# The second token mixer: latents and rotary terms worked in PSUM, squares summed by products alone, and a later begin of GpSimd's share

## The chip, the cores and the metric

The kernel runs on one core of one Trainium2 chip. The metric is the device time of the whole program in microseconds (us). A core has five engines that matter here: TensorE (PE, matrix products, with its weight loads as PEld), VectorE (DVE), ScalarE (ACT), GpSimd (POOL), and SyncE (SP), whose queue issues the loads of the weights. SBUF is the large on-chip memory that all of them use; PSUM holds what TensorE writes, in eight banks of 128 partitions x 512 fp32 values, and VectorE and ScalarE can read and write it too.

## The reference, cut to what matters

256 tokens of width 1024 go through two blocks of a network. The change lies in the token mixer of the second block:

```python
def token_mixer(h, cos, sin, w_in, conv_w, conv_b, conv_norm_g, conv_norm_b, w_conv_out,
                q_norm_g, w_uq, kv_norm_g, w_ukv, w_attn_out, w_out):
    z = h @ w_in                       # 2048 + 384 + 256 + 64 + 2048 columns
    u_glu, q_lat, kv_lat, k_r, gate_logits = jnp.split(z, IN_SPLIT, axis=-1)
    ua, ub = jnp.split(u_glu, 2, axis=-1)
    u = causal_depthwise_conv(ua * jax.nn.sigmoid(ub), conv_w, conv_b)      # 31 taps
    u = jax.nn.silu(layer_norm(u, conv_norm_g, conv_norm_b))
    y_a = u @ w_conv_out
    q = (rms_norm_2(q_lat, q_norm_g) @ w_uq).reshape(...)                   # 8 heads, 128 + 64
    kv = (rms_norm_2(kv_lat, kv_norm_g) @ w_ukv).reshape(...)
    q_rope, k_rope = apply_rope(q_rope, cos, sin), apply_rope(k_r, cos, sin)
    o = mla_attention(q_nope, q_rope, k_nope, k_rope, v)
    y_b = o @ w_attn_out
    g_a, g_b = jnp.split(jax.nn.sigmoid(gate_logits), N_BRANCHES, axis=-1)
    return (g_a * y_a + g_b * y_b) @ w_out
```

`rms_norm_2` of a latent needs, for each token, the sum of its squares over the latent's width (384 or 256); the layer norm needs the sum and the sum of squares over 1024.

## The kernel before, in words

All activations lie with the features on the 128 partitions and the 256 tokens along the row, so a latent of width 384 is three tiles of 128x256, one of 256 is two.

**Weights.** Every weight is cut into tiles of 128x128, eight tiles to a chunk of 512 KB, loaded one chunk at a time by SyncE's queue. Each chunk is split (`Weights.split`, L185 and L186) into a high part `hi` (ScalarE) and a low part `lo` = raw - hi, made either by VectorE or by GpSimd: `ws.share` is the share of chunks whose `lo` GpSimd takes. Each tile then gives three products of 256 columns: xl by hi, xh by lo, xh by hi, where xh and xl are the two parts of the activations. The helpers `mm` (L365), `act` (L362), `stt` (L353), `tt` (L350), `ts` (L357, L359) record every operation under their own lines.

**Order.** Code is written in one stream and a scheduler orders each engine's queue by it. `after(n, fn)` puts `fn` behind n more weight tiles; a list of background work, the 8 x 31 taps of the convolution, is dealt out at 0.8 taps to a weight tile (`TAP_RATE`). A tap is one VectorE operation that adds into a PSUM bank (tile `cva`; the last of a block of channels writes `cv` to SBUF).

**The mixer** (`mixer2`). Three blocks of the gated part are first multiplied with unmodulated activations (`gemm_fold`), while the modulation (tile `mod`, on VectorE, then `xh` on ScalarE and `xl` on VectorE, L353) is prepared. Then come the 48 weight tiles of the latents: two banks with two latent tiles each, and a third with the last latent tile and the rotary part of the keys. `epi_lat` copies each bank to SBUF (`lat`, `krt`). After the third bank ScalarE squares the latents (`lsq`), GpSimd adds the squares of the three and of the two tiles (L1566), and `lat_stats`, 20 tiles later (`AFTER_LAT`), sums them over the partitions with products by a column of ones (tile `sums`) and works two chains of small VectorE operations for the reciprocal roots. `lat_bc`, 56 tiles after, spreads these over the partitions (tile `dg`, product `bcps`, copy `bc` in SBUF), multiplies the latents (`lat`) and splits them into `lath` (ScalarE) and `latl` (VectorE). Meanwhile TensorE works at the 80 tiles of the rest of the gated part. The products with w_uq and w_ukv need `lath` and `latl`. The rotary terms of the keys and of two pairs of query blocks go through `rope_pair`: a product by a permutation (tile `rope`), times sin into `rt`, the source times cos in place, and their sum (`krt`, `qr`).

**Attention** follows by heads: scores (`att`), the causal mask added by a product, the maximum on VectorE (`mx`), exponentials on ScalarE, `rc` and `p` on VectorE or ScalarE, a transpose (`pt`), a copy (`pT`), and the product with the values (`o`); the products of the gate (`gate`) stand between the heads. Last, the **layer norm** of the convolved tile `cv` runs beside the gate's products: `ln2` subtracts the mean, squares four tiles of 128x512 (`Sums.square`, ScalarE), adds them on GpSimd (L262), folds the rest on VectorE and sums by two products. fp32 products (the sums, `bcps`) have two records each in the trace.

Of the kernel before, what the change touches and what calls it, by code (L numbers as in the profile page):

```python
# [9 lines left out]
F32 = mybir.dt.float32  # L10
# [4 lines left out]
AF = mybir.ActivationFunctionType  # L15
ALU = mybir.AluOpType
AX = mybir.AxisListType

P = 128
T = 256  # L20
# [7 lines left out]
EPS = 1e-6  # L28
# [8 lines left out]
AFTER_ROPE = 4  # L37
# [9 lines left out]
SC_ATT = 1.0 / math.sqrt(192.0)  # L47
# [225 lines left out]
class Kern:  # L273
# [1176 lines left out]
    def mixer2(self, xs, sums, nxt):  # L1450
        nc = self.nc
        h = self.h
        flat = lambda ap: ap.rearrange("p a t -> p (a t)")
        v2 = lambda ap: ap.rearrange("p (a t) -> p a t", a=2)
        half = lambda ps, m: ps[:, (m % 2) * T:(m % 2 + 1) * T]
        rope = {}
# [5 lines left out]
        lat = {}  # L1462
# [15 lines left out]
        latp = self.slot("lat", (P, 5, T))  # L1478
        lath, latl = self.slot("lath", (P, 5, T), F32R), self.slot("latl", (P, 5, T), F32R)
        krt = self.slot("krt", (P, 3, T))  # L1480
# [7 lines left out]
        for k in range(KD):  # L1488
            self.modulate(k, xs, self.gs[:, k:k + 1], bc4, self.shift1)

        def epi_lat(j, ps):
            if j < 2:
                self.act(latp[:, 2 * j:2 * j + 2, :], v2(ps), AF.Copy)
            else:
                self.act(latp[:, 4, :], ps[:, 0:T], AF.Copy)
                self.act(krt[:, 0, :], ps[:, T:2 * T], AF.Copy)


        up = [self.slot("up", (P, 4, 32 + T)) for _ in range(2)]
# [46 lines left out]
        for m in range(NFOLD):  # L1546
            za, zb = self.mid("za", (P, T)), self.mid("zb", (P, T))
            for j, z in ((1, zb), (0, za)):
# [2 lines left out]
            self.act(za, za, AF.Identity, bias=bias[:, 2 * m:2 * m + 1])  # L1551
            glu(m, zb, za)
        self.bg_rate = TAP_RATE
        self.ws.share = 1.0
        self.gemm(X, range(KD), [[lambda k, c=c: win(k, c) for c in (2048, 2176)],
                                 [lambda k, c=c: win(k, c) for c in (2304, 2432)],
                                 [lambda k: win(k, 2560), kr_src]], epi_lat, kouter=2)
        lsq, lsqt = {}, self.slot("lsq", (P, 5, T))
        for nm, a, n in (("q", 0, 3), ("kv", 3, 2)):
            lsq[nm] = flat(lsqt[:, a:a + n, :])  # L1560
            self.act(lsq[nm], flat(latp[:, a:a + n, :]), AF.Square)

        for nm, n in (("q", 3), ("kv", 2)):
            for i in range(1, n):
                o = lsq[nm][:, 0:T]
                nc.gpsimd.tensor_tensor(out=o, in0=o, in1=lsq[nm][:, i * T:(i + 1) * T], op=ALU.add)  # L1566

        def lat_stats():
            for nm, n in (("q", 3), ("kv", 2)):
                lat[nm] = self.rstd_tok([lsq[nm][:, 0:T]], n * P, EPS)  # L1570

        def lat_bc():
            bcs = [self.bcast(lat[nm], act=True) for nm in ("q", "kv")]
            for bc, a, n in zip(bcs, (0, 3), (3, 2)):
                for i in range(a, a + n):
                    g = self.pv("qn", i) if i < 3 else self.pv("kvn", i - 3)
                    z = latp[:, i, :]
                    self.stt(z, z, g, bc, ALU.mult, ALU.mult)
                    self.split(lath[:, i, :], latl[:, i, :], z)

        self.after(AFTER_LAT[0], lat_stats)
        self.after(AFTER_LAT[1], lat_bc)

        def x2(k):
# [8 lines left out]
        qn, qr = self.slot("qn"), self.slot("qr", (P, 4, T))  # L1593
# [9 lines left out]
            a = 2 * (i - 8)  # L1603
            return ("w_uq_2", 0, k * P, P, 0, ((a * 192 + 128, 64), ((a + 1) * 192 + 128, 64)))

        def rope_pair(dst, src, n):

            ps = self.bank("rope")
            for i in range(n):
                self.mm(ps[:, i * T:(i + 1) * T], self.cst("perm", 128), src[:, i, :])  # L1610
            t = self.mid("rt", (P, 2, T,), F32)
            cb = lambda a: a.unsqueeze(1).to_broadcast([P, n, T])
            self.tt(t[:, 0:n, :], ps[:, 0:n * T].rearrange("p (a t) -> p a t", a=n), cb(rope["sin"]), ALU.mult)
            self.tt(src, src, cb(rope["cos"]), ALU.mult)
            self.tt(dst, src, t[:, 0:n, :], ALU.add)

        def epi_qr(j, ps):
            t = self.mid("qrt", (P, 2, T,), F32)
            self.act(t, v2(ps), AF.Copy, scale=SC_ATT)
            self.after(AFTER_ROPE, lambda: rope_pair(qr[:, 2 * j:2 * j + 2, :], t, 2))  # L1620

        rope_pair(krt[:, 1:2, :], krt[:, 0:1, :], 1)
        kr = krt[:, 1, :]
        self.gemm(L(0), range(3), [[lambda k, i=i: uq(k, i) for i in (2 * j, 2 * j + 1)] for j in range(4)],
                  copied(qn, SC_ATT), kouter=0)
        self.gemm(L(0), range(3), [[lambda k, i=i: uq(k, i) for i in (8 + 2 * j, 9 + 2 * j)] for j in range(2)],
                  epi_qr, kouter=0)
        self.gemm(L(3), range(2), [[lambda k, i=i: full("w_ukv_2", 0, k, i * 256) for i in (2 * j, 2 * j + 1)]
                                   for j in range(4)], copied(kn), kouter=0)
# [111 lines left out]

        def ln2():
            mb = self.bcast(ln["mu"])
            sm = Sums(self)
            for j in range(4):
                c = cv[:, 2 * j:2 * j + 2, :]
                self.tt(c, c, self.rb(mb), ALU.subtract)
                sm.square(flat(c))
            ln["sm"] = sm
# [14 lines left out]
        for n, f in zip(AFTER_LN, (ln1, ln2, ln3, ln4)):  # L1764
            self.after(n, f)
# [351 lines left out]
```

## Time and profile before

| | |
|---|---|
| median of 3 runs | 1136.71 us (1135.8 to 1138.26) |
| profiled execution, its own time | 1137.48 us |
| its span, first to last instruction | 1135.7 us |
[...]
| busy: PE, PEld | 1099.3 us (97%), 1034.1 us (91%) |
| busy: DVE, ACT, POOL | 839.2 us (74%), 574.4 us (51%), 163.6 us (14%) |
| stretch of the mixer that the change touches | about 684 to 880 us |

The span is the profiled time less 1.8 us that lie around it. A wait is idle time of an engine just before an instruction, with the instruction that released it behind an arrow. [...] An average over the whole span hides that the engines take turns in being waited for; the rows further below are therefore taken from single stretches.

### The profile page before, as it was taken

How to read it: one execution, taken by the hardware profiler on the slowest of the kernel's cores; microseconds unless marked ns; L12 is line 12 of the kernel's file. 1: busy time of each engine (PE TensorE's matmuls, PEld its weight loads, DVE VectorE, ACT ScalarE, POOL GpSimd, SP SyncE). 2: the span in 40 equal slices, each digit the busy share in tenths (PEclk: the TensorE clock that was granted, in tenths of full speed). 3: DMA queues.
4: the chain of work that ended last, by engine and by line, in shares of the span. 5: the costliest groups of instructions: out<-in, count | busy, mean ns of one | idle time of the engine just before them, and what ended most of it. 6: DMA issues, size and time to landing. Idle time of an engine off the chain costs nothing. (4 is left out here: it accounts for less than half of the span.)

```text
span 1135.7 us, 22677 instructions
## 1 busy us (share of the span) xinstructions
PE 1099.3 (97%) x9248; PEld 1034.1 (91%) x9248; DVE 839.2 (74%) x1550; ACT 574.4 (51%) x922; POOL 163.6 (14%) x127
## 2 busy tenths in 40 slices
PE   9999999999999998999999998899899999999997
PEld 7899999999877688999999998897798999999886
DVE  6879898557964847888875579699886956965444
ACT  5664445445632546654454556454544655755342
POOL 1020000020000112100000015776363000000000
PEclk9999999999999979999999999899899998999999
DMA  8578898654432401688875544454244552655552
GB/s 300 161 244 306 309 333 261 198 174 130 135 114 75 147 3 39 206 310 300 269 216 185 186 149 140 153 159 129 70 132 152 178 170 94 188 185 173 189 190 79
DMA packets 57817, 202.52 MB, mean 178 GB/s; under 512 B 6896, under 2 KB 8560, under 8 KB 57712
## 3 DMA queue, kind: packets, MB, share of 16 engines
q1 hardware_dynamic: 57712, 201.07, 54.2%
q8 instruction: 72, 1.18, 0.4%
q14 instruction: 33, 0.27, 0.1%
HBM read 199.98 MB, written 1.05 MB: 177 GB/s over the span
## 5 line engine op out<-in xcount | busy, mean ns | idle before, releaser
L185 ACT ACTIVATE hi<-raw 128x1024 fp32r<-128x1024 f32 (+1 forms) x310 | 322.4, 1048 | 269.0 <-PE ps L365 175.2
L186 DVE TENSOR_TENSOR lo<-raw,hi 128x1024 fp32r<-128x1024 f32 (+1 forms) x268 | 327.8, 1227 | 151.3 <-ACT hi L185 150.3
L365 PE MATMUL ps<-xl,hi 128*128 128x256 f32 x1104 | 314.0, 285 | 3.7 <-DVE xl L353 3.7
L365 PE MATMUL ps<-xh,hi 128*128 128x256 f32 x1104 | 315.8, 286 | 0.5 <-ACT hi L185 0.5
L365 PE MATMUL ps<-xh,lo 128*128 128x256 f32 x1104 | 311.6, 283 | 0.8 <-DVE lo L186 0.8
L365 PEld LDWEIGHTS ps<-xl,hi 128*128 128x128 f32 x1104 | 210.5, 191 | 4.8 <-DVE xl L353 4.3
L365 PEld LDWEIGHTS ps<-xh,lo 128*128 128x128 f32 x1104 | 210.7, 191 | 1.7 <-DVE lo L186 1.6
L365 PEld LDWEIGHTS ps<-xh,hi 128*128 128x128 f32 x1104 | 209.4, 190 | 2.3 <-ACT hi L185 1.7
L186 POOL TENSOR_TENSOR lo<-raw,hi 128x1024 fp32r<-128x1024 f32 x42 | 100.9, 2415 | 86.2 <-ACT hi L185 49.6
L353 DVE SCALAR_TENSOR_TENSOR cva<-up,cwh,cva 128x256 f32<-128x256 f32 x232 | 103.3, 482 | 3.2 <-ACT cva L362 1.1
L365 PE MATMUL ps<-zl,hi 128*128 128x256 f32 x352 | 99.6, 283 | 0.0
L365 PE MATMUL ps<-zh,lo 128*128 128x256 f32 x352 | 99.4, 282 | 0.0
L365 PE MATMUL ps<-zh,hi 128*128 128x256 f32 x352 | 98.7, 280 | 0.0
L262 POOL TENSOR_TENSOR sq<-sq 128x512 f32<-128x512 f32 x17 | 23.4, 1379 | 461.5 <-ACT sq L362 461.3
L353 DVE SCALAR_TENSOR_TENSOR ada<-ada,cb 128x1024 f32<-128x1024 f32 x48 | 58.7, 1222 | 15.0 <-DMA ada<-in_ada_dram 14.9
L365 PEld LDWEIGHTS ps<-zh,hi 128*128 128x128 f32 x352 | 66.9, 190 | 0.0
L365 PEld LDWEIGHTS ps<-zh,lo 128*128 128x128 f32 x352 | 66.1, 188 | 0.0
L365 PEld LDWEIGHTS ps<-zl,hi 128*128 128x128 f32 x352 | 65.8, 187 | 0.0
L362 ACT ACTIVATE s<-z 128x256 f32<-128x256 f32 x44 | 18.4, 417 | 75.7 <-DVE z L350 75.7
L365 PE MATMUL ps<-hi,zl 128*128 128x256 f32 (+1 forms) x160 | 56.1, 350 | 0.0
L365 PE MATMUL ps<-hi,zh 128*128 128x256 f32 (+1 forms) x160 | 56.0, 350 | 0.0
L365 PE MATMUL ps<-lo,zh 128*128 128x256 f32 (+1 forms) x160 | 55.9, 350 | 0.0
(438 smaller groups left out, 2242.9 us busy)
## 6 DMA issues: line engine op xcount, KB each, us to landing
raw<-in_w_dram SPq DMA_DIRECT2D x325, 512.0 KB
ada<-in_ada_dram SPq DMA_DIRECT2D x48, 512.0 KB
h<-in_x_dram SPq DMA_DIRECT2D x8, 128.0 KB
cb<-in_c_dram SPq DMA_DIRECT2D x2, 512.0 KB
out_dram<-ht SPq DMA_DIRECT2D x3, 256.0 KB
raw<-in_w_dram SPq DMA_DIRECT2D x2, 256.0 KB
cstt<-in_cst_dram SPq DMA_DIRECT2D x1, 448.5 KB
poolw<-in_poolw_dram SPq DMA_DIRECT2D x1, 256.0 KB
```

Source lines behind the costliest of these rows:

```text
L185: self.nc.scalar.activation(out=hi[:, s], in_=raw[:, s], func=AF.Copy)
L186: eng.tensor_tensor(out=lo[:, s], in0=raw[:, s], in1=hi[:, s].bitcast(F32), op=ALU.subtract)
L262: e.tensor_tensor(out=self.parts[0], in0=self.parts[0], in1=self.parts[-1], op=ALU.add)
L353: self.nc.vector.scalar_tensor_tensor(out=out, in0=a, scalar=s, in1=b, op0=op0, op1=op1, **k)
L362: self.nc.scalar.activation(out=out, in_=a, func=f, **k)
L365: self.nc.tensor.matmul(out=out, lhsT=lhsT, rhs=rhs, start=start, stop=stop, skip_group_check=True)
```

## The change

1. `epi_lat` squares the latents straight from their banks (`lsq<-ps`), on ScalarE, in three operations beside the copies, where two operations squared the copies later. VectorE also works the keys' rotary part times cos from the bank (`krt[2]`).
2. GpSimd's share of the low parts begins 20 weight tiles later; the first three that it had go to VectorE.
3. GpSimd's three additions of squares go. `lat_stats` sums all five tiles by ten products into one bank, and works one chain of small operations on four columns.
4. `lat_bc` uses one bank for both spreads and no copies of it; the multiplied latents go to three PSUM banks (`z`), from which `lath` and `latl` are made.
5. `rope_pair` multiplies by sin in the PSUM bank itself; the source times cos (`qrc`) is worked from the bank in `epi_qr`.
6. `ln2` keeps its four tiles of squares and sums them by 16 products; three additions on GpSimd and one on VectorE go.

```diff
+        lsq = self.slot("lsq", (P, 5, T))
         def epi_lat(j, ps):
             if j < 2:
+                self.act(lsq[:, 2 * j:2 * j + 2, :], v2(ps), AF.Square)
                 self.act(latp[:, 2 * j:2 * j + 2, :], v2(ps), AF.Copy)
             else:
+                self.act(lsq[:, 4, :], ps[:, 0:T], AF.Square)
                 self.act(latp[:, 4, :], ps[:, 0:T], AF.Copy)
                 self.act(krt[:, 0, :], ps[:, T:2 * T], AF.Copy)
+                self.tt(krt[:, 2, :], ps[:, T:2 * T], rope["cos"], ALU.mult)
...
-        self.ws.share = 1.0
+        self.after(20, lambda: setattr(self.ws, "share", 1.0))
...
-        lsq, lsqt = {}, self.slot("lsq", (P, 5, T))
-        for nm, a, n in (("q", 0, 3), ("kv", 3, 2)):
-            lsq[nm] = flat(lsqt[:, a:a + n, :])
-            self.act(lsq[nm], flat(latp[:, a:a + n, :]), AF.Square)
-        for nm, n in (("q", 3), ("kv", 2)):
-            for i in range(1, n):
-                o = lsq[nm][:, 0:T]
-                nc.gpsimd.tensor_tensor(out=o, in0=o, in1=lsq[nm][:, i * T:(i + 1) * T], op=ALU.add)
         def lat_stats():
-            for nm, n in (("q", 3), ("kv", 2)):
-                lat[nm] = self.rstd_tok([lsq[nm][:, 0:T]], n * P, EPS)
+            ps = self.bank("sums")
+            for i in range(5):
+                x = 0 if i < 3 else 2
+                for tt in range(2):
+                    self.mm(ps[:, x + tt:x + tt + 1], lsq[:, i, tt * P:(tt + 1) * P], self.cst("onec", 1),
+                            i == 0 and tt == 0, i in (2, 4))
...
+            lat["qkv"] = self.rsqrt(m, [P, 4], "n4")
         def lat_bc():
-            bcs = [self.bcast(lat[nm], act=True) for nm in ("q", "kv")]
-            for bc, a, n in zip(bcs, (0, 3), (3, 2)):
-                for i in range(a, a + n):
-                    g = self.pv("qn", i) if i < 3 else self.pv("kvn", i - 3)
-                    z = latp[:, i, :]
-                    self.stt(z, z, g, bc, ALU.mult, ALU.mult)
-                    self.split(lath[:, i, :], latl[:, i, :], z)
+            ps = self.bank("bcps")
...
+            for js in ((0, 1), (2, 3), (4,)):
+                z = self.bank("z")
+                for i in js:
+                    g, bc = (self.pv("qn", i), ps[:, 0:T]) if i < 3 else (self.pv("kvn", i - 3), ps[:, T:2 * T])
+                    self.stt(half(z, i), latp[:, i, :], g, bc, ALU.mult, ALU.mult)
+                    self.split(lath[:, i, :], latl[:, i, :], half(z, i))
...
-            t = self.mid("rt", (P, 2, T,), F32)
-            cb = lambda a: a.unsqueeze(1).to_broadcast([P, n, T])
-            self.tt(t[:, 0:n, :], ps[:, 0:n * T].rearrange("p (a t) -> p a t", a=n), cb(rope["sin"]), ALU.mult)
-            self.tt(src, src, cb(rope["cos"]), ALU.mult)
-            self.tt(dst, src, t[:, 0:n, :], ALU.add)
+            o = ps[:, 0:n * T].rearrange("p (a t) -> p a t", a=n)
+            self.tt(o, o, rope["sin"].unsqueeze(1).to_broadcast([P, n, T]), ALU.mult)
+            self.tt(dst, srcc, o, ALU.add)
...
-            sm = Sums(self)
+            sm = Sums(self, direct=True)
```

Three places in the queues show what moves. The first is GpSimd's queue from the start of the mixer to the layer norm, first before, then changed; `lo` is the low part of a chunk of weights, `csum` and `sq` belong to the layer norm.

```order
L186 TENSOR_TENSOR lo<-raw,hi 128x1024 x12
L1566 TENSOR_TENSOR lsq<-lsq 128x256 x3
L186 TENSOR_TENSOR lo<-raw,hi 128x1024 x15
L1534 TENSOR_TENSOR csum<-cv 128x512
L186 TENSOR_TENSOR lo<-raw,hi 128x1024 x4
L1534 TENSOR_TENSOR csum<-csum,cv 128x512
L186 TENSOR_TENSOR lo<-raw,hi 128x1024 x11
L262 TENSOR_TENSOR sq<-sq 128x512 x3
```

```order
L186 TENSOR_TENSOR lo<-raw,hi 128x1024 x21
L1539 TENSOR_TENSOR csum<-cv 128x512
L186 TENSOR_TENSOR lo<-raw,hi 128x1024 x8
L1539 TENSOR_TENSOR csum<-csum,cv 128x512
L186 TENSOR_TENSOR lo<-raw,hi 128x1024 x10
```

The squares' additions are gone, and 39 low parts stand where there were 42. The second place is VectorE's queue behind the modulation, where the folded blocks are finished (`zb`, `za`, `up`) and the first taps begin; before, then changed.

```order
L350 TENSOR_TENSOR za<-fold,bc 128x256
L353 SCALAR_TENSOR_TENSOR up<-zb,za 128x256
L350 TENSOR_TENSOR zb<-fold,bc 128x256
L353 SCALAR_TENSOR_TENSOR up<-zb,za 128x256
L350 TENSOR_TENSOR za<-fold,bc 128x256
L353 SCALAR_TENSOR_TENSOR cva<-up,cwh,cva 128x256 x2
L353 SCALAR_TENSOR_TENSOR up<-zb,za 128x256
L353 SCALAR_TENSOR_TENSOR cva<-up,cwh,cva 128x256 x45
```

```order
L350 TENSOR_TENSOR za<-fold,bc 128x256
L353 SCALAR_TENSOR_TENSOR up<-zb,za 128x256
L186 TENSOR_TENSOR lo<-raw,hi 128x1024
L353 SCALAR_TENSOR_TENSOR up<-zb,za 128x256
L350 TENSOR_TENSOR zb<-fold,bc 128x256
L350 TENSOR_TENSOR za<-fold,bc 128x256
L353 SCALAR_TENSOR_TENSOR cva<-up,cwh,cva 128x256
L186 TENSOR_TENSOR lo<-raw,hi 128x1024
L353 SCALAR_TENSOR_TENSOR up<-zb,za 128x256
L353 SCALAR_TENSOR_TENSOR cva<-up,cwh,cva 128x256
L186 TENSOR_TENSOR lo<-raw,hi 128x1024
L353 SCALAR_TENSOR_TENSOR cva<-up,cwh,cva 128x256 x46
```

Three low parts now stand among the last `up` and the first taps, all behind the modulation's `mod` and `xl`. The third place is VectorE's queue where the latents are scaled and split, before and changed, from the first scaling on; `pvt` holds the gains.

```order
L353 SCALAR_TENSOR_TENSOR lat<-lat,pvt,bc 128x256
L353 SCALAR_TENSOR_TENSOR cva<-up,cwh,cva 128x256
L353 SCALAR_TENSOR_TENSOR lat<-lat,pvt,bc 128x256
L353 SCALAR_TENSOR_TENSOR cva<-up,cwh,cva 128x256
L350 TENSOR_TENSOR latl<-lat,lath 128x256
```

```order
L353 SCALAR_TENSOR_TENSOR z<-lat,pvt,bcps 128x256
L353 SCALAR_TENSOR_TENSOR cva<-up,cwh,cva 128x256
L353 SCALAR_TENSOR_TENSOR up<-tb,ps 128x256
L353 SCALAR_TENSOR_TENSOR cva<-up,cwh,cva 128x256
L350 TENSOR_TENSOR latl<-z,lath 128x256
```

The order stays much the same; what changes is that each scaling and each split has one operand in PSUM (`bcps`, `z`). On TensorE the products of `sums` move from behind 240 weight products of the mixer to behind 201, and number ten where there were four.

## Rows read from the trace of the kernel before

**Rows 1.** The waits of PE, 680 to 900 us: total us, times, longest us.
```profile
PE sums L365 <- POOL lsq L1566: 5.0, 1, 5.0
PE ps L365 <- DVE xl L353: 3.7, 2, 2.5
PE o L365 <- ACT pT L362: 3.3, 1, 3.3
PE sums L365 <- DVE sq L350: 2.5, 1, 2.5
PE pt L368 <- ACT p L362: 1.3, 1, 1.3
PE ps L365 <- DVE rt L350: 0.9, 1, 0.9
```

**Rows 2.** Table by stretch: length, busy of PE, PEld, DVE, ACT, POOL, clock, DMA.
```profile
690.00:700.00 10.00, 7.52 (x51) 7.32 (x50) 9.71 (x27) 5.80 (x12) 1.61 (x1) 0.83 0.20 57
700.00:720.00 20.00, 20.00 (x170) 20.00 (x170) 18.63 (x46) 10.34 (x13) 19.56 (x9) 1.00 0.60 182
...
725.00:730.00 5.00, 4.24 (x20) 4.24 (x21) 2.49 (x16) 0.00 (x0) 1.39 (x2) 0.50 0.36 115
800.00:810.00 10.00, 9.03 (x36) 7.55 (x37) 7.53 (x21) 4.38 (x13) 0.52 (x1) 0.52 0.14 52
870.00:875.00 5.00, 4.93 (x29) 4.96 (x30) 2.12 (x6) 1.46 (x2) 1.95 (x10) 0.66 0.32 105
```

**Rows 3.** Groups on VectorE, 684 to 700 us, by shape: busy us, mean ns.
```profile
L353 DVE SCALAR_TENSOR_TENSOR mod<-h,gs,bc 128x256 f32<-128x256 f32 x8 | 7.6, 1005 | 0.0
L353 DVE SCALAR_TENSOR_TENSOR xl<-mod,xh 128x256 fp32r<-128x256 f32 x8 | 3.4, 474 | 0.0
...
L186 DVE TENSOR_TENSOR lo<-raw,hi 128x1024 fp32r<-128x1024 f32 x1 | 1.2, 1226 | 0.3 <-ACT hi L185 0.3
```

**Rows 4.** Timeline of GpSimd, 700 to 727 us.
```profile
700.44 21.27 POOL L186 TENSOR_TENSOR lo<-raw,hi 128x1024 fp32r<-128x1024 f32 x9 [8.83 <-DVE cva L353]
...
724.18 2.21 POOL L1566 TENSOR_TENSOR lsq<-lsq 128x256 f32<-128x256 f32 x3
```

**Rows 5.** Timeline of PE: sixteen records of fp32 sums (two records per product).
```profile
946.67 1.84 PE L365 MATMUL sums<-cstt,sq 128*128 128x1 f32 x16
```

**Rows 6.** Groups on VectorE, 738 to 781 us, by shape.
```profile
L350 DVE TENSOR_TENSOR latl<-lat,lath 128x256 fp32r<-128x256 f32 x5 | 6.1, 1215 | 0.0
L353 DVE SCALAR_TENSOR_TENSOR lat<-lat,pvt,bc 128x256 f32<-128x256 f32 x5 | 4.3, 862 | 0.0
L350 DVE TENSOR_TENSOR qr<-qrt,rt 128x512 f32<-128x512 f32 x2 | 3.2, 1592 | 0.0
L350 DVE TENSOR_TENSOR krt<-krt,rt 128x256 f32<-128x256 f32 x1 | 2.2, 2223 | 0.0
L350 DVE TENSOR_TENSOR krt<-krt,rope 128x256 f32<-128x256 f32 x1 | 1.8, 1757 | 0.0
...
L350 DVE TENSOR_TENSOR rt<-rope 128x512 f32<-128x512 f32 x2 | 1.4, 678 | 0.0
```

**Rows 7.** Timeline of VectorE: one operation stretched, one not.
```profile
742.85 2.53 DVE L350 TENSOR_TENSOR latl<-lat,lath 128x256 fp32r<-128x256 f32 x1
...
747.27 0.41 DVE L350 TENSOR_TENSOR latl<-lat,lath 128x256 fp32r<-128x256 f32 x1
```

**Rows 8.** Timeline of GpSimd at the first of them.
```profile
742.69 2.40 POOL L186 TENSOR_TENSOR lo<-raw,hi 128x1024 fp32r<-128x1024 f32 x1 [0.44 <-ACT hi L185]
```

**Rows 9.** The tile cva on VectorE: ns least/median/most, first and last start.
```profile
L353 DVE SCALAR_TENSOR_TENSOR cva<-up,cwh,cva x232: 469/481/491, 697.8 to 853.0; 128x256 f32<-128x256 f32 x116
```

**Rows 10.** Timeline of VectorE: the first maximum of attention.
```profile
785.91 0.28 DVE L1667 TENSOR_REDUCE mx<-att 128x1 f32<-128x128 f32 x1
```

**Rows 11.** Timeline of PE: the mask that ends the first head's scores.
```profile
777.43 0.28 PE L365 MATMUL att<-cmask 128*128 128x128 bf16 x2
```

**Rows 12.** Timeline of ScalarE, 862 to 868 us.
```profile
866.80 0.64 ACT L362 ACTIVATE sq<-cv 128x512 f32<-128x512 f32 x1 [1.47 <-POOL sq L262]
```

More of the change, by code (lines that the diff above doesn't have):

```diff
@@ L1568, in lat_stats @@
-        def lat_stats():
-            for nm, n in (("q", 3), ("kv", 2)):
-                lat[nm] = self.rstd_tok([lsq[nm][:, 0:T]], n * P, EPS)
-        def lat_bc():
-            bcs = [self.bcast(lat[nm], act=True) for nm in ("q", "kv")]
-            for bc, a, n in zip(bcs, (0, 3), (3, 2)):
-                for i in range(a, a + n):
-                    g = self.pv("qn", i) if i < 3 else self.pv("kvn", i - 3)
-                    z = latp[:, i, :]
-                    self.stt(z, z, g, bc, ALU.mult, ALU.mult)
-                    self.split(lath[:, i, :], latl[:, i, :], z)
+        def lat_stats():
+            ps = self.bank("sums")
[4 more added lines that the diff above has]
+                            i == 0 and tt == 0, i in (2, 4))
+            m = self.tiny("lm", [P, 4], tag="n4m")
+            self.ts(m[:, 0:2], ps[:, 0:2], 1.0 / (3 * P), EPS, ALU.mult, ALU.add)
+            self.ts(m[:, 2:4], ps[:, 2:4], 1.0 / (2 * P), EPS, ALU.mult, ALU.add)
+            lat["qkv"] = self.rsqrt(m, [P, 4], "n4")
@@ new lines, in lat_bc @@
+        def lat_bc():
+            ps = self.bank("bcps")
+            for x in range(2):
+                dg = self.mid("dg2", (P, T))
+                for tt in range(2):
+                    self.act(dg[:, tt * P:(tt + 1) * P], self.cst("ident", 128), AF.Copy,
+                             scale=lat["qkv"][:, 2 * x + tt:2 * x + tt + 1])
+                self.mm(ps[:, x * T:(x + 1) * T], self.cst("ones", 128), dg, x == 0, True)
+            for js in ((0, 1), (2, 3), (4,)):
[4 more added lines that the diff above has]
+                    self.split(lath[:, i, :], latl[:, i, :], half(z, i))
@@ L1604, in uq, with rope_pair @@
             return ("w_uq_2", 0, k * P, P, 0, ((a * 192 + 128, 64), ((a + 1) * 192 + 128, 64)))
-        def rope_pair(dst, src, n):
+        def rope_pair(dst, src, srcc, n):
             ps = self.bank("rope")
@@ L1610, in rope_pair @@
                 self.mm(ps[:, i * T:(i + 1) * T], self.cst("perm", 128), src[:, i, :])
-            t = self.mid("rt", (P, 2, T,), F32)
-            cb = lambda a: a.unsqueeze(1).to_broadcast([P, n, T])
-            self.tt(t[:, 0:n, :], ps[:, 0:n * T].rearrange("p (a t) -> p a t", a=n), cb(rope["sin"]), ALU.mult)
-            self.tt(src, src, cb(rope["cos"]), ALU.mult)
-            self.tt(dst, src, t[:, 0:n, :], ALU.add)
+            o = ps[:, 0:n * T].rearrange("p (a t) -> p a t", a=n)
+            self.tt(o, o, rope["sin"].unsqueeze(1).to_broadcast([P, n, T]), ALU.mult)
+            self.tt(dst, srcc, o, ALU.add)
         def epi_qr(j, ps):
-            t = self.mid("qrt", (P, 2, T,), F32)
+            t, tc = self.mid("qrt", (P, 2, T,), F32), self.mid("qrc", (P, 2, T,), F32)
             self.act(t, v2(ps), AF.Copy, scale=SC_ATT)
-            self.after(AFTER_ROPE, lambda: rope_pair(qr[:, 2 * j:2 * j + 2, :], t, 2))
-        rope_pair(krt[:, 1:2, :], krt[:, 0:1, :], 1)
+            self.stt(tc, v2(ps), SC_ATT, rope["cos"].unsqueeze(1).to_broadcast([P, 2, T]), ALU.mult, ALU.mult)
+            self.after(AFTER_ROPE, lambda: rope_pair(qr[:, 2 * j:2 * j + 2, :], t, tc, 2))
+        rope_pair(krt[:, 1:2, :], krt[:, 0:1, :], krt[:, 2:3, :], 1)
         kr = krt[:, 1, :]
```

## The prediction

> **What bounds the kernel now.** I read the table by stretch first, then the waits of TensorE, then the timelines around each wait. TensorE is the engine whose idle time becomes program time: between 700 and 720 us it is busy throughout, 170 products in 20 us or 0.118 us for one, at clock 1.00, with GpSimd busy 19.56 us of the same 20 [rows 2]. What it loses, it loses in a few places: 5.0 us for GpSimd's sums of squares, 3.7 us for `xl`, 3.3 and 1.3 us for `pT` and `p` in attention, 2.5 us for the squares of the layer norm, 0.9 us for `rt` [rows 1]. [...]
>
> Why do the waits for VectorE exist? Look at `latl`: the same operation takes 2.53 us at 742.85 and 0.41 us at 747.27 [rows 7]. During the first GpSimd makes a low part from 742.69 to 745.09, and `latl` ends 0.3 us later [rows 8]; during the second GpSimd stands still. An operation of VectorE with both inputs in SBUF is drawn out to the end of GpSimd's. The taps, which have an operand in PSUM, are not: 232 of them lie between 469 and 491 ns [rows 9], though GpSimd ran without a gap from 700.44 to 721.7 us [rows 4].
>
> **The change part by part.** Gains are subtracted from the profiled execution, 1137.48 us; the median of the runs shown is 0.8 us lower.
>
> *A, the start (share begins later).* Eight `mod` of 1.005 us, against 0.481 for a tap of the same shape, carry 8 x 0.524 = 4.2 us of stretching [rows 3, 9]; the low parts of GpSimd that cause it go to VectorE, 3 x 1.23 = 3.7 us [rows 3]. VectorE's total gains only 0.5 us, but its order matters: the three low parts stand behind all `xl`, so the wait of 3.7 us and the low clock (10 us x 0.17 = 1.7) go [rows 1, 2]. In their place TensorE soon needs what stands behind the `xl`: a bank freed by the finishing of the folded blocks, then the first low part. I bound that new wait by nothing and by the three low parts, 3.7 us, and take 1.3, about one of them. A = 3.7 + 1.7 - 1.3 = 4.1, between 1.7 and 5.4.
>
> *B, the sums of squares.* GpSimd's additions begin at 724.18 because ten low parts, the run of nine from 700.44 and one more, stand ahead of them in its queue [rows 4]. The squares now come from ScalarE alone, out of the banks; three such operations in a stretch where it is busy 10.34 of 20 us [rows 2] cost nothing, and without that cover 1.7 us (as 0.64 us for 128x512 twice and about 0.4 for the smaller [rows 12]). The products stand 39 weight products, 4.6 us, nearer to the latents, with the last square long done. So the 5.0 us go, and with them half of five microseconds at 0.50, 2.5 us [rows 1, 2]. Six more products, 12 records of 1.84/16 = 0.115 us [rows 5], cost 1.4. The two chains of small operations become one; that is VectorE's time and it shows in D. B = 5.0 + 2.5 - 1.4 = 6.1; with the products at the low clock 4.7, with none of their cost exposed 7.5.
>
> *C, latents and rotary terms.* VectorE loses its stretching between 738 and 781 us: `latl` 6.1 - 5 x 0.41 = 4.0, `lat` 4.3 - 5 x 0.481 = 1.9, the two `krt` 2.22 + 1.76 - 0.82 = 3.2, `qr` 3.2 - 1.4 = 1.8, in all 10.9 us [rows 6, 7, 9]. TensorE's wait for `rt` (0.9) goes [rows 1]; three `z` banks and the banks worked in place are held longer than before, for which I put 0.5 of new wait, between none and twice what `rt` costs now, 1.8. C = 0.4, between -0.9 and 0.9.
>
> A price speaks against this part. The trace gives none: `xl`, the same form with no PSUM operand, takes 474 ns, a tap 481 [rows 3, 9], so I put nothing. [...]
>
> *D, attention.* The first scores end on TensorE at 777.71 [rows 11], and VectorE comes to their maximum at 785.91 [rows 10]: it is 8.2 us behind, and the waits for `p` and `pT` are paid from that. With A to C TensorE gets there 10.6 us earlier, at 767.1. VectorE gets to its maximum earlier by 10.9 of stretching, 0.5 of the start, and up to 5.0 in which it too stood waiting for the sums: 769.5, a lag of 2.4 us; without the last, 7.4. The waits of 3.3 and 1.3 are what is left of a lag of 8.2 after TensorE's other work in a head, so 2.4 leaves none. Between 800 and 810 half the time is at the low level: 4.8, less half of the 0.97 us in which TensorE was idle [rows 2], is 4.3. D = 3.3 + 1.3 + 4.3 = 8.9; I take 3 as the lower end, where the lag stays near 7.4.
>
> *E, the layer norm.* The 2.5 us for the squares and 0.34 x 5 = 1.7 us of clock go [rows 1, 2]. ScalarE's last square now waited 1.47 us for GpSimd [rows 12], and will not. Fourteen more products, 28 records of 0.115, cost 3.2 [rows 5]. E = 1.0; if the records ran at the low level throughout it would be -2.2, with half of them hidden 2.6. This is the one part where the change gives back most of what it gains.
>
> The edits left over, a copy of `bc` less, `qrc` beside ScalarE's copy, are on engines that TensorE does not wait for at that place; `qrc` costs 2 x 0.68 us of VectorE [rows 6] if D's lag is wrong.
>
> Sum: 4.1 + 6.1 + 0.4 + 8.9 + 1.0 = 20.5. The profiled execution would be 1117.0, and a median that stands to it as before 1116.2.
>
> **The rivals.**
> - *VectorE stays behind.* The lag is made of its backlog of taps, and with the waits gone TensorE runs into it again. For it: VectorE is busy 18.63 of 20 us already between 700 and 720 [rows 2], and the sums now come while taps are left. Against it: the 10.9 us. D is then 3 and about 1.5 us of waits come at the latents: 20.5 - 7.4 = 13.1, 1123.6. Chance 0.2.
> - *The operations with one PSUM operand are drawn out too*, so the change does not do what it says. Against it: the taps; for it: none of the new forms (result in PSUM, two inputs with one broadcast) stands in the trace. A, B and E stay, C and D go: 11.2, 1125.5. Chance 0.08.
> - *The products of sums are dear.* They load a new 128x128 weight for one column each; at the low clock B loses 1.4 and E 3.2: 15.9, 1120.8. Chance 0.1.
> - *Slower: TensorE runs out of banks.* At the latents two banks belong to taps, one to `bcps`, three to `z`; two of eight are left, and one is filled in 48 products, 5.7 us. If VectorE frees `z` and the rotary banks later than that, each of six places gives a wait like that for `xl` in its two parts, about 2.5 us and 1.7 of clock: 25 us, more than the 20.5 gained, 1141. It decides when VectorE is more than 5.7 us behind at `bcps`. Chance 0.03.
>
> **How the numbers follow.** The forecast as summed has 0.59, with a range of its own from 1111 (every term at its better end, 25.3) to 1120 (16.7). The range from 1110 to 1125 takes in the first and third rival and leaves out about 0.15. 0.2% is 2.3 us, about what a measurement can tell. Faster: the four cases below 1126 with 0.97, less 0.02 for several of them together, 0.95; same 0.02; slower, the last case, 0.03.
>
> **What would show it.** In the trace after: no `lsq` on GpSimd, `sums` of the latents without idle time before it and with the clock at 1.00 after it; `latl`, `krt`, `qr` near 0.41 to 0.68 us whatever GpSimd does; the first `mx` within 3 us of its scores; no stretch near 0.50 in attention; `sums` of the layer norm as 32 records in about 3.7 us with no wait ahead. I am wrong if VectorE's lag at the first head is still above 5 us, or if new waits stand before weight products on banks that VectorE frees.

## The result, and the profile after

The changed kernel takes 1127.07 us (median of 4 runs, 1126.21 to 1127.99), beside 1136.4 us for the kernel before: a ratio of 0.9915, 95% interval 0.9898 to 0.9932. It is faster, by 9 us where 20.5 were forecast (1116.2), and outside the range given. The profiled execution took 1126.21 us, its span 1124.4, with a mean granted clock of 0.984 where the kernel before had 0.975; it is 11.3 us below the profiled one before, and the stretches below are taken from these two.

TensorE's waits between 680 and 900 us, in the changed kernel, answer to [rows 1]:

```profile
PE bcps L365 <- ACT dg L362: 4.4, 1, 4.4
PE ps L365 <- DVE zb L350: 1.3, 1, 1.3
PE ps L365 <- DVE qr L350: 1.2, 1, 1.2
PE o L365 <- ACT pT L362: 0.7, 1, 0.7
```

All six waits that stood there are gone or small. New are two of 1.2 to 1.3 us, for `zb` and `qr`, and one of 4.4: at `bcps`, the spread of the latents' reciprocal roots, for `dg`, which ScalarE makes from the end of VectorE's chain of small operations (`rs_y`):

```profile
734.28 1.28 ACT L362 ACTIVATE dg<-cstt,rs_y 128x128 f32<-128x128 f32 x4 [4.34 <-DVE rs_y L353]
```

The table by stretch answers to [rows 2]; the clock in it is TensorE's granted clock as a share of full speed, in the mean over the stretch:

```profile
690.00:700.00 10.00, 8.71 (x73) 8.54 (x72) 10.00 (x24) 6.97 (x13) 2.58 (x2) 1.00 0.29 98
730.00:735.00 5.00, 0.58 (x5) 0.38 (x4) 5.00 (x14) 0.72 (x3) 2.35 (x1) 1.00 0.57 185
735.00:740.00 5.00, 4.97 (x25) 4.70 (x26) 4.04 (x12) 2.06 (x5) 0.37 (x1) 0.66 0.07 26
800.00:810.00 10.00, 10.00 (x76) 8.70 (x75) 8.55 (x22) 5.75 (x15) 4.65 (x4) 1.00 0.33 105
855.00:860.00 5.00, 5.00 (x41) 5.00 (x40) 2.14 (x3) 1.14 (x2) 0.00 (x0) 0.87 0.51 163
860.00:865.00 5.00, 5.00 (x25) 5.00 (x25) 1.88 (x5) 1.46 (x2) 2.94 (x10) 0.50 0.13 50
```

The clock stays at 1.00 at the start and in attention. Between 730 and 735 us TensorE is busy 0.58 us of 5, and the clock behind that is 0.66. The last two lines are the layer norm: TensorE is busy all the time, and yet the clock is 0.87 and then 0.50.

To see where time went I took the start of five operations on TensorE's timeline of each kernel, and the differences between them: the mixer's first `bcps`, the `bcps` of the latents, the first scores, the last run of products `o`, and then, for the layer norm, from the sum for the mean to the spread of the root. The table is worked out from those starts.

| us | start to latents' spread | to first scores | to last `o` | layer norm |
|---|---|---|---|---|
| before | 54.7 | 38.5 | 57.4 | 19.7 |
| changed | 51.3 | 38.0 | 48.4 | 21.7 |
| forecast of the change | -10.2 (A, B) | -0.4 (C) | -8.9 (D) | -1.0 (E) |
| measured | -3.3 | -0.5 | -9.0 | +2.0 |

The stretches outside these have the same work in both kernels; the changed one takes 1.0 us more before the mixer and 1.5 less behind the layer norm. Attention gained what was forecast, and the layer norm lost. The first two columns have to be read with care: TensorE's records between the starts, counted on its timeline, are 346 and 269 before and 375 and 252 in the changed kernel. Of the 29 more in the first, twelve are the sums'; the other 17 are weight products, about 2.0 us at 0.119, that now stand ahead of the latents' spread instead of behind it. For the same work the first column is therefore about -5.4, half of the forecast, and the second about +1.6, near the low clock behind the spread (0.34 x 5 = 1.7 us in the table by stretch).

VectorE's timeline of the changed kernel at the chain (start, length, operation, idle before it):

```profile
721.96 0.42 DVE L350 TENSOR_TENSOR krt<-ps,rope 128x256 f32<-128x256 f32 x1 [1.57 <-ACT krt L362]
...
723.02 0.15 DVE L359 TENSOR_SCALAR lm<-sums 128x2 f32<-128x2 f32 x1
...
724.53 2.22 DVE L359 TENSOR_SCALAR rs_y<-rs_t 128x4 int32<-128x4 int32 x1
...
727.06 0.15 DVE L350 TENSOR_TENSOR rs_t<-rs_y 128x4 f32<-128x4 f32 x1
...
727.46 2.13 DVE L353 SCALAR_TENSOR_TENSOR rs_t<-rs_t,lm 128x4 f32<-128x4 f32 x1
...
730.37 2.02 DVE L350 TENSOR_TENSOR rs_t<-rs_y 128x4 f32<-128x4 f32 x1
...
734.09 0.15 DVE L353 SCALAR_TENSOR_TENSOR rs_y<-rs_t,rs_y 128x4 f32<-128x4 f32 x1
```

GpSimd's timeline beside it:

```profile
724.32 2.41 POOL L186 TENSOR_TENSOR lo<-raw,hi 128x1024 fp32r<-128x1024 f32 x1 [0.43 <-ACT hi L185]
727.17 2.41 POOL L186 TENSOR_TENSOR lo<-raw,hi 128x1024 fp32r<-128x1024 f32 x1 [0.44 <-ACT hi L185]
730.02 2.35 POOL L186 TENSOR_TENSOR lo<-raw,hi 128x1024 fp32r<-128x1024 f32 x1 [0.44 <-ACT hi L185]
```

And TensorE's:

```profile
713.31 2.29 PE L365 MATMUL sums<-cstt,lsq 128*128 128x1 f32 x20
...
735.02 0.70 PE L365 MATMUL bcps<-dg,cstt 128*128 128x256 f32 x2 [4.45 <-ACT dg L362]
```

Operations on 128x4 that take 0.15 us took 2.0 to 2.2, three times, and each ended within 0.02 us of the end of a low part of GpSimd. Two more things bear on the wait: the late begin (the sums are there at 715.6, `lm` comes at 723.02, behind taps and 1.57 us of waiting for ScalarE's `krt`) and the end at 734.24, 0.8 us ahead of `bcps`. In the kernel before, the two chains ran from 726.8 to 733.2 and none of their operations took more than 0.17 us; VectorE's, ScalarE's and GpSimd's timelines had these rows:

```profile
728.20 0.16 DVE L359 TENSOR_SCALAR rs_y<-rs_t 128x2 int32<-128x2 int32 x1
...
729.27 0.16 DVE L353 SCALAR_TENSOR_TENSOR rs_t<-rs_t,mean 128x2 f32<-128x2 f32 x1
...
733.01 0.15 DVE L353 SCALAR_TENSOR_TENSOR rs_y<-rs_t,rs_y 128x2 f32<-128x2 f32 x1
```

```profile
732.12 1.06 ACT L185 ACTIVATE hi<-raw 128x1024 fp32r<-128x1024 f32 x1 [8.07 <-issue]
```

```profile
733.26 2.41 POOL L186 TENSOR_TENSOR lo<-raw,hi 128x1024 fp32r<-128x1024 f32 x1 [6.87 <-ACT hi L185]
```

GpSimd stood still from the additions (they end at 726.39) until after the chains, because ScalarE's next high part came only at 732.12. That TensorE's stop at the sums had held this high part up is likely, as the next one waits for TensorE's products; but the profile names no releaser for the 8.07 us ("issue"), so it is not shown. If it is so, the wait that was removed had kept the chains undisturbed.

### The profile page after: what moved, and what is told of

Its sections match the earlier page's. It is cut to its first block, busy times and chain, and to the rows that moved or that the text cites. A ratio compares the mean times of both kernels' runs of the same rounds, so it can differ in the third digit from the quotient of the medians.

```text
span 1124.4 us, 22728 instructions
## 1 busy us (share of the span) xinstructions
PE 1095.4 (97%) x9288; PEld 1030.7 (92%) x9288; DVE 834.1 (74%) x1542; ACT 572.9 (51%) x921; POOL 150.8 (13%) x118
## 5 line engine op out<-in xcount | busy, mean ns | idle before, releaser
L186 DVE TENSOR_TENSOR lo<-raw,hi 128x1024 fp32r<-128x1024 f32 (+1 forms) x271 | 333.3, 1234 | 153.5 <-ACT hi L185 152.5
L186 POOL TENSOR_TENSOR lo<-raw,hi 128x1024 fp32r<-128x1024 f32 x39 | 93.8, 2418 | 86.6 <-ACT hi L185 86.5
L262 POOL TENSOR_TENSOR sq<-sq 128x512 f32<-128x512 f32 x14 | 18.9, 1357 | 455.0 <-ACT sq L362 455.0
L353 DVE SCALAR_TENSOR_TENSOR ada<-ada,cb 128x1024 f32<-128x1024 f32 x48 | 58.7, 1223 | 16.6 <-DMA ada<-in_ada_dram 16.4
```

Of the source, the lines that this page charges most:

```text
L186: eng.tensor_tensor(out=lo[:, s], in0=raw[:, s], in1=hi[:, s].bitcast(F32), op=ALU.subtract)
L262: e.tensor_tensor(out=self.parts[0], in0=self.parts[0], in1=self.parts[-1], op=ALU.add)
L353: self.nc.vector.scalar_tensor_tensor(out=out, in0=a, scalar=s, in1=b, op0=op0, op1=op1, **k)
```

## The experiments

**Three theories.** 1: GpSimd's low parts draw the chain out, and that makes the wait at `bcps`. 2: the chain is late because VectorE comes to it late. 3: in the layer norm the 32 one-column records themselves bring the clock down, and cost more than the wait that they replace. Every kernel ran on one chip with the kernel before beside it, and ratios are to that. The changed kernel's is 0.9915. The starts that the table above is made from are called marks; each kernel's are those of its own profiled execution.

**The chain in PSUM.** Every operation of the chain with two inputs gets one of them in PSUM (two more operations, for second copies of y):

```diff
-            lat["qkv"] = self.rsqrt(m, [P, 4], "n4")
+            t, yp = ps[:, 8:12], ps[:, 16:20]
+            r, y, p = (self.tiny(n, [P, 4], tag=n, bufs=1) for n in ("lr", "ly", "lp"))
+            self.ts(t.bitcast(U32), m.bitcast(U32), 1, None, ALU.logical_shift_right)
+            for o in (y, yp):
+                self.ts(o.bitcast(I32), t.bitcast(I32), -1.0, RS_MAGIC, ALU.mult, ALU.add)
+            self.tt(t, y, yp, ALU.mult)
...
```

> The changed kernel with the latents' chain of small operations worked with one operand of each in PSUM (two operations more), all else the same. Theory 1 (GpSimd's low parts draw the chain out): three of its ten operations took 2.22, 2.13 and 2.02 us instead of about 0.15; without that the chain ends some 5.7 us sooner, before TensorE gets to bcps, so the wait of 4.45 us and the low clock behind it (1.7 us) go: 1127.1 - 6.1 = about 1121. Theory 2 (the chain is late because VectorE comes to it late, behind taps and a wait for ScalarE): it begins as late as before, at most 1 us is gained, 1126 to 1127.

Measured: 1106.91 us, ratio 0.9732 (0.9719 to 0.9745). That is 20 us faster than the changed kernel, where theory 1 asked for 6. A gain three times too large is no confirmation. The marks showed why: the first `bcps` of the mixer already came 9.3 us sooner, in a stretch whose instructions are the same in both. What differed there was the address of the tiles: three small tiles more had moved every tile of the later phases by 96 bytes. So I ran the chain again in small tiles that exist already (tags "n4t", "n4y", "rsp"), which moves nothing:

> The chain in PSUM as in e1_chain_in_psum, but with the small tiles that the kernel has already, so that every large tile keeps its address. e1_chain_in_psum was 20 us faster than the changed kernel, of which its trace shows 5.2 us between the first spread of the mixer and the first scores, and the rest in stages in which both kernels have the same instructions; its three new small tiles had moved all tiles of the phases by 96 bytes. If theory 1 (the chain is drawn out) is worth about 5 to 6 us and the rest was the move by 96 bytes, this kernel takes 1121 to 1122. If the rest too came from the chain, it takes 1107. If theory 2 holds, 1127.

Measured: 1120.67 us, ratio 0.984 (0.9814 to 0.9865). TensorE's waits from 680 us on in this kernel:

```profile
PE o L365 <- ACT pT L362: 1.4, 1, 1.4
PE ps L365 <- DVE zb L350: 1.3, 1, 1.3
PE ps L365 <- DVE qr L350: 0.9, 1, 0.9
```

Its chain on VectorE and the spread on TensorE:

```profile
723.48 0.15 DVE L359 TENSOR_SCALAR lm<-sums 128x2 f32<-128x2 f32 x1
...
729.59 0.15 DVE L353 SCALAR_TENSOR_TENSOR rs_y<-sums,rs_t 128x4 f32<-128x4 f32 x1
```

```profile
731.84 0.59 PE L365 MATMUL bcps<-dg,cstt 128*128 128x256 f32 x2
```

GpSimd still makes its low parts beside it:

```profile
727.63 2.41 POOL L186 TENSOR_TENSOR lo<-raw,hi 128x1024 fp32r<-128x1024 f32 x1 [0.44 <-ACT hi L185]
```

The chain begins as late as in the changed kernel (723.48 against 723.02), lasts 6.3 us instead of 11.2, and the wait at `bcps` is gone. From the start to the first scores it takes 82.6 us where the changed kernel takes 89.4 and the one before 93.1; the forecast's A, B and C asked for 82.5. Theory 1 holds.

**Without the wait for ScalarE ahead of the chain.** The keys' product by cos is taken from SBUF, beside the rotary product.

```diff
-                self.tt(krt[:, 2, :], ps[:, T:2 * T], rope["cos"], ALU.mult)
...
+        self.tt(krt[:, 2, :], krt[:, 0, :], rope["cos"], ALU.mult)
         rope_pair(krt[:, 1:2, :], krt[:, 0:1, :], krt[:, 2:3, :], 1)
```

> The changed kernel with the keys' product by cos not taken from the bank ahead of the chain but from SBUF beside the rotary product. Theory 2: VectorE no longer stands 1.57 us for ScalarE's copy just ahead of the chain, so the chain and bcps come 1.6 us sooner: about 1125. Theory 1: the same three operations are still caught by low parts of GpSimd and the chain ends where one of those ends; no more than 0.5 us, 1126.6 to 1127.1, or slower by up to 2 where the product in SBUF is drawn out itself.

Measured: 1127.0 us (1123.36 to 1130.04), ratio 0.9907 (0.9892 to 0.9922). Counted from the sums, the chain began 2.0 us sooner than in the changed kernel (7.7 us behind them against 9.7) and ended only 0.5 us sooner: four of its operations were now drawn out, to 1.81, 2.08, 2.13 and 2.02 us. The latents' spread came 0.5 us sooner, the first scores 1.9 us later after it, with a new wait of 1.1 us for `qrc`. So the late begin by itself is worth half a microsecond, and nothing in the whole time.

**GpSimd's share at once** (part 2 undone):

```diff
-        self.after(20, lambda: setattr(self.ws, "share", 1.0))
+        self.ws.share = 1.0
```

> The changed kernel with GpSimd's share begun at once (part 2 undone). If term A is right, the wait for xl of 3.7 us and 1.7 us of clock come back and 1.5 us of new waits go: 3.9 us slower, about 1131. Rival: what is won at the start is only stood out at bcps, where TensorE waits for VectorE's chain in any case; then nothing, 1127, with a shorter wait at bcps.

Measured: 1129.12 us (1126.75 to 1131.27), ratio 0.9921 (0.9908 to 0.9934). The ratio is 0.0006 above the changed kernel's, less than 1 us, and the intervals overlap. The marks are clearer. The waits for `xl` are back:

```profile
PE ps L365 <- DVE xl L353: 3.7, 2, 2.5
PE bcps L365 <- ACT dg L362: 3.3, 1, 3.3
```

From the start to the products of the latents' sums, 230 records in both kernels, it takes 33.3 us against 29.6, and to the first scores 93.5 against 89.4. So term A is there, 3.7 us where it acts, though as a time of the whole kernel it is not settled.

**The layer norm's additions back** (part 6 undone):

```diff
-            sm = Sums(self, direct=True)
+            sm = Sums(self)
```

> The changed kernel with the layer norm's squares added on GpSimd and VectorE again (part 6 undone). Theory 3 (the 32 records of sums cost 4.13 us against 0.58, and the clock falls behind them, 3.4 us in three stretches): undoing gives 3.55 + 3.4 back and takes the wait of 2.5 and its 1.7 us of clock: 2.7 us faster, about 1124.3. The forecast's term E: 1.0 us slower, about 1128.1.

Measured: 1126.05 us, ratio 0.9899 (0.9887 to 0.9912); the whole time leaves it open, the layer norm's stretch does not: 19.8 us against 21.7. In these two executions part 6 costs 1.9 us.

**The sums of the layer norm spread**: the same 16 products, in four groups of four, three weight tiles apart.

```diff
...
+                for i in range(4):
+                    self.after(n - 9 + 3 * i, lambda i=i: ln_part(i))
...
```

> The changed kernel with the 16 products of the layer norm's sums in four groups of four, three weight tiles apart, instead of one run. Theory 3a (the run of 32 one-column records, 4.13 us, brings the clock down although TensorE never stands idle): between the spread of the mean and the spread of the root the clock stays at 1.00 and the two stages take 10.1 + 11.6 - 3.3 = 18.4 us; about 1124. Theory 3b (the clock falls there for another reason): 21.7 us as in the changed kernel, 1127.

Measured: 1124.69 us, ratio 0.9879 (0.9861 to 0.9897). TensorE's timeline and, for the time behind the sums, the table by stretch in this kernel:

```profile
851.48 0.95 PE L365 MATMUL sums<-cstt,sq 128*128 128x1 f32 x8
...
857.36 0.95 PE L365 MATMUL sums<-cstt,sq 128*128 128x1 f32 x8
```

```profile
858.00:860.00 2.00, 2.00 (x18) 2.00 (x18) 0.50 (x3) 0.55 (x1) 0.76 (x4) 1.00 0.88 254
860.00:862.00 2.00, 2.00 (x19) 2.00 (x18) 1.23 (x1) 0.51 (x1) 1.67 (x5) 1.00 0.06 16
```

In the changed kernel the same 32 records stood in one run:

```profile
855.70 4.13 PE L365 MATMUL sums<-cstt,sq 128*128 128x1 f32 x32
```

Spread, they take 4 x 0.95 = 3.8 us, the clock stays at 1.00, and the stretch takes 18.6 us, within 0.2 of the expectation. That speaks for theory 3a, that the unbroken run and not the number of its products lowered the clock, but it does not settle it. Eight of the kernels profiled have the unbroken run. In seven the clock fell behind it (in e2_krt_later later and for a shorter time, and the stretch took 20.1 us). From the sums for the mean to the kernel's last sums it took 94.5 us in the changed kernel, in e4_share_at_once and in f1_chain_in_psum_same_places and 92.9 in e2_krt_later, against 91.6 with the sums spread; in e1_chain_in_psum it took 92.1, against 87.9 with the sums spread in the other kernel that is moved by 96 bytes and has its chain in PSUM (g2_chain_psum_spread_moved). In g3_after_moved_64_bytes and g4_after_moved_32_bytes the 256-column products behind the run took 0.41 us, as they do in the changed kernel at clock 0.50, where those ahead of it took 0.28. In f2_after_moved_96_bytes, shown further below, the clock did not fall:

```profile
851.09 3.63 PE L366 MATMUL sums<-cstt,sq 128*128 128x1 f32 x32
```

```profile
851.00:856.00 5.00, 5.00 (x47) 5.00 (x46) 1.90 (x5) 0.66 (x2) 0.43 (x3) 1.00 0.65 205
856.00:861.00 5.00, 5.00 (x43) 4.95 (x42) 2.03 (x3) 2.82 (x6) 2.48 (x8) 1.00 0.29 102
```

There the run takes 3.63 us, 0.113 for a record, and the stretch 18.6 us, as with the sums spread. With the sums spread the clock stayed up in both kernels that have them. So behind the unbroken run the low clock comes often and not always; what decides is open.

**Chain in PSUM and the additions back**, without moving a tile:

> f1_chain_in_psum_same_places with the layer norm's squares added on GpSimd again. Theory 1 and 3 together: 1121.5 less 1.9, as the two stages are apart: about 1119.5. If the wait taken away in the latents only comes back in attention, as the forecast's first rival has it, 1125 or more.

Measured: 1120.65 us, ratio 0.9843 (0.9821 to 0.9864). This is a miss: no faster than the chain in PSUM alone. To the first scores it took 84.1 us and in the layer norm 21.2, where the parts alone had 82.6 and 19.8. The gain in the latents did not come back as waits in attention (49.0 us in both), so that part of the question has its answer. The 1.5 us in the latents lie in the clock behind the run of 20 records of the latents' sums, here:

```profile
715.00:720.00 5.00, 5.00 (x37) 5.00 (x37) 5.00 (x14) 1.21 (x2) 2.02 (x2) 0.79 0.73 208
720.00:725.00 5.00, 5.00 (x39) 5.00 (x39) 1.93 (x6) 1.60 (x3) 3.25 (x2) 0.87 0.34 108
```

TensorE had no wait there. In the ten microseconds from these sums on, the mean clock is 0.83 in four of the eleven kernels run that have them (e1_chain_in_psum, f2_after_moved_96_bytes, this one and g3_after_moved_64_bytes) and 1.00 in the other seven and in the changed kernel, with the same ten products: a loss of 1.7 us that comes or not. The layer norm's 1.4 us are its clock too (0.50 and 0.87 from 855 and from 860 us, five each, where e3_ln_adds_on_gpsimd had 1.00 and 0.66); why it stayed low longer here than in e3_ln_adds_on_gpsimd is open.

**The address.** An unused small tile ahead of the phases' tiles, and nothing else (one memset):

```diff
         self.tp = self.pool("tiny", 3)
+        self.nc.vector.memset(self.tp.tile([P, 24], F32, tag="pad", name="pad", bufs=1), 0.0)
```

> The changed kernel with one unused small tile of 96 bytes ahead, which moves the tiles of the phases by 96 bytes; no other instruction but one memset. If the address is what made the rest of e1_chain_in_psum's gain, about 14 us: 1113. If it was something else, 1127.

> The kernel before, with the unused small tile of 96 bytes. If the address sets the pace of products whatever the change, some 14 us less than before: about 1123. If the move helps only the changed kernel, 1137.

Measured: 1112.7 us, ratio 0.9779 (0.9757 to 0.9802), and for the kernel before 1120.43 us, ratio 0.9843 (0.9818 to 0.9869). So the move works without the change too, and is worth more than it. Not all of its 14 us on the changed kernel is pace: in the profiled execution 3.1 us are the layer norm's clock that stayed up, and 1.7 went the other way in the latents. One line by stretch of the changed kernel, and the same line of the moved one, in the first block of the network where both have the same work and TensorE no wait:

```profile
205.00:255.00 50.00, 50.00 (x419) 50.00 (x418) 24.72 (x24) 20.97 (x22) 4.20 (x3) 1.00 0.61 195
```

```profile
205.00:255.00 50.00, 50.00 (x444) 50.00 (x443) 27.44 (x23) 21.89 (x23) 7.40 (x4) 1.00 0.63 196
```

At the same clock TensorE does 444 products instead of 419, 0.113 us for one instead of 0.119. The kernel before does 419 in the same stretch, and by the addresses that the two programs assign, both kernels of the case have the phases' tiles 64 bytes past a multiple of 128, so their comparison is not touched by this. Which remainder counts, I tried by two other sizes of the unused tile, 16 and 8 columns:

> The changed kernel with an unused small tile of 64 bytes. If what counts is the address by 64 bytes (the tiles of the phases now begin at a multiple of 64, and lay 32 beyond one in the moved kernels), this changes nothing: 1127. If any move helps, 1113.

> The changed kernel with an unused small tile of 32 bytes. If the address by 64 bytes counts, this does what the move by 96 bytes did: 1113. If it takes 96, 1127.

Measured: 1124.05 us, ratio 0.9874 (0.9857 to 0.9892), and 1125.03 us, ratio 0.9885 (0.9869 to 0.9901). The move by 32 bytes did not do what 96 did, so the theory of a remainder by 64 falls. Both do 424 products in the stretch shown above, and gain 2 to 5 us at most on the changed kernel. Which rule lies behind it stays open.

**All together**: the chain in PSUM without new tiles, the spread sums, and the unused 96 bytes.

> The three things that helped, together: the chain in PSUM without new tiles, the layer norm's sums spread, and the move by 96 bytes. By the runs so far: 1127.1 less 6.4 (chain), 14.4 (move) and up to 3.3 (spread, if theory 3a holds; 0 by 3b, and little if the clock recovers sooner at the new addresses): 1103 to 1106. If two of them were the same time counted twice, 1110 or more.

Measured: 1102.4 us (1101.27 to 1103.49), ratio 0.9683 (0.9668 to 0.9697): 3.2% faster than the kernel before, and less than every other kernel here. Its marks are 82.4 us to the first scores, as in the kernel with the chain alone, 49.0 in attention and 18.6 in the layer norm. The last stands in the moved kernel without the spread too, so in this combination the spread sums are not shown to add anything.

## Why the prediction was wrong

- **Term A was right.** The waits for `xl` are gone, the new wait for `zb` is 1.3 us, and the clock is 1.00. That 1.3 was put in is partly luck: it was a choice between nothing and 3.7. With the share at once the stretch from the start to the sums is 3.7 us longer; A was 4.1.
- **Term B failed**, at the sentence "The two chains of small operations become one; that is VectorE's time and it shows in D." The products of the sums did as forecast. But the chain behind them is on TensorE's path at `bcps`, and the operations in it have their inputs in SBUF, as the `latl` of [rows 7] have. I priced the stretching for the operations that had shown it before, and not for those that had been spared because GpSimd stood still beside them. It cost 4.45 us of wait and 1.7 of clock, 6.1 together, which is all of B by chance. With the chain in PSUM, A, B and C together come to what was forecast, to 0.1 us.
- **Term C was right in its mechanism; that the table shows its size is chance**: in that column 17 products fewer (2.0 us) and the 1.7 of low clock, which belong to the spread ahead of it, nearly cancel. With the chain in PSUM the clock stays up (0.12 us to a product from 732.93 on, behind the spread), 25 weight products (3.0 us) have moved, and of the 3.5 us that the column gains about 0.5 is left for C, where 0.4 was forecast. `latl` took 0.42 us, `krt` 0.43, `qr` 0.69 in the mean, with GpSimd busy beside `krt`, both `qr` and one of the five `latl` (740.59). The group of each on VectorE, 737 to 775 us, answers to [rows 6]:

```profile
L353 DVE SCALAR_TENSOR_TENSOR z<-lat,pvt,bcps 128x256 f32<-128x256 f32 x5 | 2.4, 486 | 0.0
L350 DVE TENSOR_TENSOR latl<-z,lath 128x256 fp32r<-128x256 f32 x5 | 2.1, 422 | 0.0
...
L350 DVE TENSOR_TENSOR qr<-qrc,rope 128x512 f32<-128x512 f32 x2 | 1.4, 685 | 0.0
```

  The price that was weighed for a PSUM operand did not show either: `latl` takes 0.42 us with one and 0.41 without [rows 7].
- **Term D was right**, 9.0 against 8.9, though by two misses that cancel. The first scores end at 774.92, the maximum starts at 777.04: a lag of 2.1 us, where 2.4 was worked out. But TensorE came there 2.8 us sooner, not 10.6, and VectorE 8.9 sooner, not 16.4. With the chain in PSUM, where TensorE does come as early as forecast (10.5 us sooner, counted from the mixer's first `bcps`), the lag is 1.6 us and attention 0.6 us longer than in the changed kernel, so the term holds there within 0.6. No run undoes parts 4 and 5, so what shortened the lag is read from the traces and not tested.

```profile
774.64 0.28 PE L365 MATMUL att<-cmask 128*128 128x128 bf16 x2
```

```profile
777.04 0.28 DVE L1678 TENSOR_REDUCE mx<-att 128x1 f32<-128x128 f32 x1
```

- **Term E had the wrong sign**: 1.0 gained was forecast, 2.0 lost was measured. The wait of 2.5 and its 1.7 of clock went, and the records cost 3.55 (4.13 less the 0.58 of four), but with the run of them came a low clock, 3.4 us (0.13 and 0.50 of the two stretches of five shown above, and 0.2 in the next; half a microsecond of it is in the 4.13 already). The step that failed is the one that put no clock loss behind the records: I took it from [rows 2], where TensorE had idle time in each stretch below 1.00, that a low clock needs an idle TensorE ahead of it. Where the clock stayed up behind the same unbroken run, in f2_after_moved_96_bytes, the stretch is 1.1 us shorter than before, and E had 1.0. So the rest of the term was right; when the low clock comes is open.
- Of the rivals the first named the right engine and the wrong reason: VectorE was late at the latents, not for its backlog of taps but for GpSimd, and attention was not touched. The rival that put the products at the low clock had 3.2 us for the layer norm, near the 3.0 by which E missed, and that is luck: the run itself took 4.13 us where it takes 3.63 at 1.00, and most of the loss lay in the products behind it.
- **The range** had its slow end at 16.7 us, which is worked out from no terms; the lower ends of the five terms add up to 6.3, or 1130 us, and the measured time lies inside that.

## What to carry to other kernels

When a wait goes, ask what it had kept apart: look up which engines stood still during it, and price the operations behind it as if those engines ran. In these kernels the products of one column that only sum stood better between wide products than in one run: behind the run of 32 records the clock fell in seven of eight kernels, behind the groups of eight in none of two. And before a gain is put down to an edit, see that tiles elsewhere have kept their addresses: a control that moves them and changes nothing else costs one run.

## What the runs showed of the hardware

- Three operations of VectorE on 128x4 took 2.02 to 2.22 us beside a low part on GpSimd, against 0.15. Each began 0.2 to 0.4 us behind the start of a low part and ended within 0.02 us of its end. Two of them, at 727.46 and 730.37, have both inputs in SBUF. The third, `rs_y` at 724.53, reads a single SBUF tile; in e2_krt_later another of that kind, on 32-bit integers too, took 1.81. Why a single input was drawn out as well, no run here shows. In f1_chain_in_psum_same_places, with one operand of each two-input operation in PSUM, none of the chain took more than 0.17 us beside the low parts from 724.78 and 727.63.
- TensorE's clock fell behind an unbroken run of 32 one-column records with no idle time in seven of eight kernels profiled, to 0.50 in the changed kernel between 860 and 865 us, and behind four groups of eight, 0.95 us each in g1_ln_sums_spread, in none of two. Behind the run of 20 records (2.29 us) of the latents' sums it fell in four kernels of twelve, to a mean of 0.83 over ten microseconds.
- A move of the phases' tiles by 96 bytes in SBUF shortened the time of a product from 0.119 to 0.113 us between 205 and 255 us, at clock 1.00; moves of 32 and 64 bytes gave 0.118.
